# Attention scores in a one-core trunk kernel: two query blocks at a time, each on 64 rows of TensorE, in three products instead of two

## The chip, the cores and the metric

The kernel runs on one core of one Trainium2 chip, in one launch. The metric is the device time of that launch in microseconds (us), lower is better. The engines are named as the profile names them: PE is TensorE's matmul, PEld its weight load, DVE is VectorE, ACT is ScalarE, POOL is GpSimd, SP is the engine whose queue issues the DMAs here.

## The reference, cut to what matters

The model is one layer over a sequence of 2048 rows of width 1024: a wide input projection, a convolution branch, an attention branch of 8 heads of 64, and two output projections. The change lies in the attention branch alone:

```python
z = jnp.einsum("bqhd,bkhd->bhqk", qb, kb, preferred_element_type=jnp.float32) * scale
mask = s_idx < t_idx
log_beta = jax.nn.log_sigmoid(z)
log_1m_beta = jnp.where(mask, log_beta - z, 0.0)
suffix = lax.cumsum(log_1m_beta, axis=3, reverse=True) - log_1m_beta
weights = jnp.where(mask, jnp.exp(log_beta + suffix), 0.0)
outs.append(jnp.einsum("bhqk,bkhd->bqhd", weights.astype(v.dtype), vb))
```

Every score z = q.k is over 64 numbers. The weight of a key is its sigmoid times the product of one minus the sigmoids of the keys between it and the query.

## The kernel before

**Precision.** Every float32 operand is split into a high part (a cast to `float32r`, the matmul format) and a low part (the rest), and a product is made from high times high, high times low and low times high. A dense product (`mm3`) is three matmuls for each 128 rows of contraction.

**Stages.** The first projects the input (x normalised, transposed and split) into q, k, v, the convolution's input and most gates, normalises the heads and writes q and k to DRAM, head by head and in chunks of 512 rows: tiles `qst` and `kst` of 128 x 512, where partitions 0 to 63 hold the high part of the 64 numbers and 64 to 127 the low part. The second stage is the attention, with dense matmuls of the remaining gates put between (the "fill", tile `pd`). The third makes the output projections (tiles `p` and `po`).

**The attention stage.** It goes over 80 units (head h, query chunk rc, key chunk g, with g from rc to 3; the sequence is stored reversed). 32 units are diagonal (g equal to rc), where only the keys from a block's own column on count; 48 are off the diagonal. A unit has four query blocks (qb 0 to 3) of 128 queries, against 512 keys. For each block:

- `z_stage` makes the scores on PE in one PSUM bank (tile `z`, three banks): two matmuls of 128 contraction rows. `q1` holds [high; low] of the queries and `q2` [low; high], both against `kt`, [high; low] of the keys. The first gives high x high + low x low, the second low x high + high x low: all four products. On the diagonal the matmuls are 512, 384, 256 and 256 columns wide for the blocks 0 to 3.
- ACT makes the sigmoid (`w`, seven buffers) and the sigmoid of the negated score (back into `z`), DVE a running product along the keys (`sc`, a scan that reads `z` and so holds its bank), POOL multiplies it into `w`.
- One unit later `av_stage` (called `T(kb)` in the unit's loop) transposes the four `w` of a key block on PE (`pT`), ACT and DVE split them into `thi` and `tlo`, and `av_mm` (`AV(kb)`) multiplies them with the values into `av`.

**What sets the order.** From the stage before on, `pin[0]` is true, and PE keeps the order in which the program calls it. In a unit that order is Z(0), fill, the last AV of the unit before, fill, Z(1), T(3), fill, T(2), fill, Z(2), fill, AV(3), T(1), Z(3), AV(2), T(0), fill, AV(1); `others` puts in as many steps of the fill (three matmuls each) as a table of due times says. ACT, DVE, POOL and the DMA queue of SP are ordered by the scheduler. All loads and stores of the stage are issued by SP, in order.

**Loads.** `load_q` brings q for one (h, rc) by three DMAs, one chunk ahead; two buffers. `kt` and `vt` are loaded at the first query chunk of a head (rc equal to 0) and used by all units of that key chunk.

Of the kernel before, what the change touches and what calls it, by code (L numbers as in the profile page):

```python
# [8 lines left out]
F32 = mybir.dt.float32  # L9
F32R = mybir.dt.float32r  # L10
# [9 lines left out]
P = 128  # L20
# [3 lines left out]
CH = 512  # L24
# [6 lines left out]
HD = 64  # L31
# [15 lines left out]
def f(ap):  # L47
    return ap.bitcast(F32)
# [3 lines left out]
def trunk_kernel(  # L52
# [20 lines left out]
    nc = tc.nc  # L73
# [6 lines left out]
    def dram(name, shape, dt):  # L80
        return dp.tile(shape, dt, name=name, tag=name)
# [27 lines left out]
    def load_piece(pool, src):  # L109
        hi = pool.tile([P, 1024], F32R, tag="whi", name="whi")  # L110
        lo = pool.tile([P, 1024], F32R, tag="wlo", name="wlo")
        split_into(src, hi, lo)
        return hi, lo
# [3 lines left out]
    def mm(*a, **k):  # L117
        i = nc.tensor.matmul(*a, **k)  # L118
        if pin[0]:
            tc.keep_in_program_order(i)  # L120
# [36 lines left out]
    kst_d = [[dram(f"kst{h}_{g}", [P, CH], F32) for g in range(NCH)] for h in range(NH)]  # L157
    qst_d = [[dram(f"qst{h}_{g}", [P, CH], F32) for g in range(NCH)] for h in range(NH)]
# [29 lines left out]
    def hT(g):  # L188
        return hT_[g]
# [10 lines left out]
    with ExitStack() as s1:  # L200
# [221 lines left out]
        with tc.tile_pool(name="hx", reuse_waits="tile", bufs=1) as hx:  # L422
# [88 lines left out]
            for kc in range(KC):  # L511
# [10 lines left out]
                hi, lo = (h[kc] for h in hT(g0))  # L522
# [28 lines left out]
            def first(w2):  # L551
                return [nat_tile(pd, w2, g0, half) for half in range(2)]
# [12 lines left out]
            h = h_chunk(ORDER[1], hx, (), xs)  # L565
# [4 lines left out]
            k1 = first(w2_k1)  # L570
# [5 lines left out]
            h = h_chunk(ORDER[2], hx, (0, 4))  # L576
# [319 lines left out]
    with ExitStack() as s2:  # L896
        at = s2.enter_context(tc.tile_pool(name="at", reuse_waits="tile", bufs=1, side="right"))
        pd = s2.enter_context(tc.tile_pool(name="pd2", reuse_waits="tile", bufs=2, space=PSUM))
        pz = s2.enter_context(tc.tile_pool(name="pz", reuse_waits="tile", bufs=3, space=PSUM))
# [37 lines left out]
        kt, vt = {}, {}  # L937
        st = {}

        def load_q(h, rc):  # L940
            q1 = at.tile([P, CH], F32R, tag="q1", name="q1", bufs=2)
            q2 = at.tile([P, CH], F32R, tag="q2", name="q2", bufs=2)
            nc.sync.dma_start(f(q1), qst_d[h][rc])
            nc.sync.dma_start(f(q2[0:HD]), qst_d[h][rc][HD:P])
            nc.sync.dma_start(f(q2[HD:P]), qst_d[h][rc][0:HD])
            st[h, rc] = {"q": (q1, q2), "w": {}}

        def z_stage(h, rc, g, qb):
            diag = g == rc
            if qb == 0:  # L950
                if rc == 0:
                    kt[g] = at.tile([P, CH], F32R, tag=f"kt{g}", name=f"kt{g}")
                    nc.sync.dma_start(f(kt[g]), kst_d[h][g])
                    vt[g] = at.tile([P, 4, P], F32R, tag=f"vt{g}", name=f"vt{g}")
                    nc.sync.dma_start(f(vt[g]), vst_d[h][g])
                if diag:
                    nxt = (h, rc + 1) if rc + 1 < NCH else (h + 1, 0)
                    for hr in ((h, rc), nxt) if n_ == 0 else (nxt,):
                        if hr[0] < NH:
                            load_q(*hr)  # L960
            s_ = st[h, rc]
            q1, q2 = s_["q"]
            lo = qb * P if diag else 0
            zlo = min(lo, 256)
            qs = slice(qb * P, (qb + 1) * P)
            z = pz.tile([P, CH], F32, tag="z", name="z")
            mm(z[:, zlo:], q1[:, qs], kt[g][:, zlo:], start=True, stop=False)
            mm(z[:, zlo:], q2[:, qs], kt[g][:, zlo:], start=False, stop=True)
            w = at.tile([P, CH], F32, tag="w", name="w", bufs=7)
            nc.scalar.activation(out=w[:, lo:], in_=z[:, lo:], func=AF.Sigmoid, scale=HD ** -0.5)  # L970
            nc.scalar.activation(out=z[:, lo:], in_=z[:, lo:], func=AF.Sigmoid,  # L971
                                 scale=-HD ** -0.5)
            s = sc[qb]
            if not diag:
                nc.vector.tensor_tensor_scan(  # L975
                    out=s[:, 1:], data0=z, data1=w, initial=s[:, 0:1],
                    op0=ALU.mult, op1=ALU.bypass)
            else:
                nc.vector.tensor_tensor_scan(  # L979
                    out=s[:, lo + 1:], data0=z[:, lo:], data1=tri[:, :CH - lo], initial=1.0,  # L980
                    op0=ALU.mult, op1=ALU.max)
            nc.gpsimd.tensor_tensor(out=w[:, lo:], in0=w[:, lo:], in1=s[:, lo:CH], op=ALU.mult)  # L982
            if diag:
                nc.gpsimd.affine_select(
                    out=w[:, lo:lo + P], in_=w[:, lo:lo + P], pattern=[[1, P]],
                    compare_op=ALU.is_gt, fill=0.0, base=0, channel_multiplier=-1)
            if g < NCH - 1:
                nc.gpsimd.tensor_copy(s[:, 0:1], s[:, CH:CH + 1])
            s_["w"][g, qb] = w
# [23 lines left out]
        def av_mm(h, rc, g, kb, v_, n, av, thi, tlo):  # L1013
            mm(av[:, :n], v_[:, kb, :], thi[:, :n],
                             start=(g == rc and kb == 3), stop=False)
            mm(av[:, :n], v_[:, kb, :], tlo[:, :n],
                             start=False, stop=(g == NCH - 1 and kb == 0))
            if g == NCH - 1 and kb == 0:
                lo_, hi_ = slice(0, HD), slice(HD, P)
                a, b = (lo_, hi_) if h % 2 == 0 else (hi_, lo_)  # L1020
                oc = at.tile([P, CH], F32, tag="fsg", name="oc", bufs=2)
                nc.scalar.copy(out=oc[a], in_=av[b])
                nc.vector.tensor_tensor(out=oc[a], in0=av[a], in1=oc[a], op=ALU.add)
                nc.sync.dma_start(o_d[h // 2][rc][a], oc[a])
# [109 lines left out]
        units = [(h, rc, g) for h in range(NH) for rc in range(NCH) for g in range(rc, NCH)]  # L1134
# [26 lines left out]
        for n_, u in enumerate(units + [None]):  # L1161
            r = [None] * 4
            p = prev[0] if prev else None

            def T(kb):
                if p:
                    r[kb] = av_stage(*p, kb, prev[1])

            def AV(kb):
                if p:  # L1170
                    av_mm(*p, kb, prev[1], *r[kb])

            def Z(qb):
                if u is not None:
                    z_stage(*u, qb)

            def others(q, half):

                nonlocal nf, ny, ygen, wr, yp
                while nf < (int(due[2 * q + half + 1] + 0.001) if q < LAST else NF):  # L1180
                    next(fill)
                    nf += 1
                if early and not half:
                    steps, quarter, f_, a = early[0]
                    if (nf >= steps and q % 2 == 0) if quarter == 0 else q >= quarter:
                        early.pop(0)

                        with tc.high_priority(offset=-60):
                            f_(a)
                if q == LAST - 8 and not half:  # L1190
                    wcs[0] = load_piece(wpa, w_cs[0])
                if q == LAST and not half:
                    hst.close()
                    wr = s3.enter_context(tc.tile_pool(name="wr", reuse_waits="tile", bufs=1))
                    yp = s3.enter_context(tc.tile_pool(name="yp", reuse_waits="tile", bufs=1))
                    with tc.high_priority(offset=0):
                        wo[0] = load_piece(wpa, w_out[0])
                    z0_ = [zt[kc] for kc in range(2 * JC)]
                    ygen = y_tiles(0, halves(z0_[:JC]), halves(z0_[JC:]), lambda n: psum(n), y)
                if q >= LAST:  # L1200
                    next(ygen)
                    ny += 1

            Z(0)
            others(4 * n_, 0)
            if held:
                av_mm(*held)
            others(4 * n_, 1)
            Z(1)
            T(3)  # L1210
            others(4 * n_ + 1, 0)
            T(2)
            others(4 * n_ + 1, 1)
            Z(2)
            others(4 * n_ + 2, 0)
            AV(3)
            T(1)
            Z(3)
            AV(2)
            T(0)  # L1220
            others(4 * n_ + 2, 1)
            others(4 * n_ + 3, 0)
            others(4 * n_ + 3, 1)
            AV(1)
            held = (*p, 0, prev[1], *r[0]) if p else None
            prev = (u, vt[u[2]]) if u is not None else None
# [73 lines left out]
```

## Time and profile before

| what | value |
|---|---|
| runs of the kernel before | 1830.12, 1831.95, 1835.28 us, median 1831.95 |
| the profiled execution | 1829.36 us, its span 1827.6 us |
| PE busy, share of the span | 97% |
| attention stage (first to last score) | 783 to 1485 us of the span |
| score matmuls | 640, in 160 pairs of two query blocks |
| DMA over the attention stage | 93 GB/s, mean busy share 0.31 |

How to read it: times in a view are microseconds from the start of the span, single instructions in nanoseconds where a column says ns. A matmul's duration is longer than the time by which it holds up the next one, since matmuls are pipelined and their ends are modelled, so what a matmul costs is read from start to start. "128*128 128x512" is a weight of 128 x 128 and a moving operand of 128 partitions by 512 columns. In the timeline "x2" joins two like instructions, from the start of the first to the end of the last. An arrow "<-" behind an idle time names what ended it.

### The profile page before, as it was taken

The page shows a single profiled execution, that of the slowest core. Times are in us where ns is not written, and L with a number is a line of the kernel's source. Part 1 is how long each engine was busy: PE and PEld are TensorE (multiplying, and loading weights), DVE is VectorE, ACT ScalarE, POOL GpSimd, SP SyncE. Part 2 cuts the span into 40 slices and gives each one's busy share as a digit, 9 for nine tenths or more (in the row PEclk, how much of TensorE's full clock was granted, in tenths as well). Part 3 has the DMA queues.
Part 4 walks back from the last instruction along what each step waited for, and adds up shares of the span by engine and source line. Part 5 has one row for each costly group of instructions (what it writes and reads, how often), then busy time and mean ns, then how long its engine had stood idle before and what let it go on. Part 6 is the DMA issues. An engine that isn't in the chain of part 4 may idle for free.

```text
span 1827.6 us, 27222 instructions
## 1 busy us (share of the span) xinstructions
PE 1773.7 (97%) x9612; PEld 1507.4 (82%) x9612; DVE 1231.1 (67%) x1696; ACT 833.2 (46%) x1960; POOL 659.2 (36%) x819
## 2 busy tenths in 40 slices
PE   6899999999999999999999999999999999999999
PEld 5888889899898888878888888887787777888887
DVE  7656577987879555567777787877778785334341
ACT  5465113222131143367777777777777652010100
POOL 0253112102111133366666666666666721010100
PEclk9999999999999999999999999999999999999999
DMA  8563411415133454342232323232324346353532
GB/s 295 174 190 104 139 35 53 121 37 165 41 101 102 145 179 144 132 133 85 78 100 72 105 72 99 63 100 73 96 76 156 95 136 213 104 162 99 169 95 81
DMA packets 117597, 211.08 MB, mean 115 GB/s; under 512 B 15442, under 2 KB 27730, under 8 KB 117460
## 3 DMA queue, kind: packets, MB, share of 16 engines
q1 hardware_dynamic: 116308, 207.24, 36.8%
q10 hardware_dynamic: 1152, 2.10, 0.3%
q8 instruction: 76, 1.25, 0.3%
q14 instruction: 61, 0.50, 0.1%
HBM read 137.98 MB, written 71.30 MB: 115 GB/s over the span
## 4 chain that ended last, share of the span: by engine, by line
PE 77%; DVE 7%; POOL 4%; issue 4%; DMA 4%; ACT 3%; SPq 0%; ACTq 0%; DVEq 0%; POOLq 0%
PE pd L118 44%; PE po L118 9%; PE p L118 9%; PE av L118 5%; PE pT L123 5%; PE z L118 4%; POOL w L982 3%; DVE sc L975 2%; DVE tlo L1009 1%; ACT z L971 1%; PE pt L123 1%; DMA wl<-in_w_cs_dram 1%; POOL wlo L106 1%; DMA wl<-in_w_qkv_dram 1%; DMA qst<-qhi 1%
## 5 line engine op out<-in xcount | busy, mean ns | idle before, releaser
L982 POOL TENSOR_TENSOR w<-w,sc 128x512 f32<-128x512 f32 (+1 forms) x320 | 362.0, 1133 | 235.0 <-DVE sc L975 175.6
L118 PE MATMUL pd<-hh,whi 128*128 128x512 f32 x1024 | 326.1, 400 | 0.0
L975 DVE TENSOR_TENSOR_SCAN sc<-z,sc,w 128x512 f32<-128x512 f32 x192 | 244.2, 1277 | 74.3 <-ACT z L971 73.5
L106 POOL TENSOR_TENSOR wlo<-wl,whi 128x512 fp32r<-128x512 f32 x88 | 131.6, 1506 | 407.3 <-ACT whi L105 406.3
L970 ACT ACTIVATE w<-z 128x512 f32<-128x512 f32 (+1 forms) x320 | 171.8, 537 | 126.5 <-PE z L118 102.4
L118 PEld LDWEIGHTS pd<-hh,whi 128*128 128x128 f32 x1024 | 183.7, 189 | 31.1
L118 PE MATMUL pd<-hhi,whi 128*128 128x512 f32 x512 | 208.3, 407 | 1.0 <-ACT vsg L882 1.0
L1009 DVE TENSOR_TENSOR tlo<-pT,thi 128x512 fp32r<-128x512 f32 (+1 forms) x320 | 186.0, 598 | 30.0 <-ACT thi L1008 27.0
L118 PE MATMUL pd<-hhi,wlo 128*128 128x512 f32 x512 | 200.4, 391 | 0.0
L118 PE MATMUL pd<-hlo,whi 128*128 128x512 f32 x512 | 200.3, 391 | 0.0
L118 PE MATMUL pd<-hh,wlo 128*128 128x512 f32 x512 | 200.1, 391 | 0.0
L118 PE MATMUL z<-kt,q 128*128 128x512 f32 (+2 forms) x640 | 190.9, 379 | 0.0
L123 PE MATMUL pT<-ident,w 128*128 128x128 f32 x1088 | 174.7, 274 | 7.8 <-POOL w L982 6.2
L1008 ACT CAST thi<-pT 128x512 fp32r<-128x512 f32 (+1 forms) x320 | 165.6, 526 | 36.1 <-PE pT L123 33.0
L123 PEld LDWEIGHTS pT<-ident,w 128*128 128x128 f32 x1088 | 136.7, 140 | 47.2 <-POOL w L982 14.4
L971 ACT ACTIVATE z<-z 128x512 f32<-128x512 f32 (+1 forms) x320 | 171.8, 537 | 0.0
L979 DVE TENSOR_TENSOR_SCAN sc<-z,tri 128x512 f32<-128x512 f32 (+3 forms) x128 | 104.3, 820 | 58.4 <-ACT z L971 38.0
L105 ACT CAST whi<-wl 128x512 fp32r<-128x512 f32 x88 | 53.8, 623 | 163.9 <-PE pd L118 135.4
L118 PE MATMUL av<-tlo,vt 128*128 128x512 f32 (+1 forms) x320 | 120.3, 376 | 8.2 <-DVE tlo L1009 7.8
L118 PEld LDWEIGHTS z<-kt,q 128*128 128x128 f32 x640 | 109.7, 189 | 14.7 <-DVE sc L979 0.3
L118 PE MATMUL av<-thi,vt 128*128 128x512 f32 (+1 forms) x320 | 116.7, 365 | 0.0
L118 PEld LDWEIGHTS pd<-hhi,wlo 128*128 128x128 f32 x512 | 96.4, 188 | 20.9
(289 smaller groups left out, 3553.6 us busy)
## 6 DMA issues: line engine op xcount, KB each, us to landing
wl<-in_w_in_dram SPq DMA_DIRECT2D x64, 256.0 KB, 3.0
wa<-in_w_ada_dram SPq DMA_DIRECT2D x24, 512.0 KB, 5.5
wl<-in_w_qkv_dram SPq DMA_DIRECT2D x36, 256.0 KB, 2.8
xt<-in_x_n_dram SPq DMA_DIRECT2D x16, 512.0 KB, 5.5
vst<-st SPq DMA_DIRECT2D x64, 128.0 KB, 2.0
kt<-kst SPq DMA_DIRECT2D x32, 256.0 KB, 2.8
vt<-vst SPq DMA_DIRECT2D x32, 256.0 KB, 2.6
q<-qst SPq DMA_DIRECT2D x32, 256.0 KB, 2.9
```

The source lines that it names most:

```text
L105: nc.scalar.copy(out=hi[:, s], in_=wl)
L106: (lo_eng or nc.gpsimd).tensor_tensor(out=lo[:, s], in0=wl, in1=f(hi[:, s]), op=ALU.subtract)
L118: i = nc.tensor.matmul(*a, **k)
L123: i = nc.tensor.transpose(*a)
L970: nc.scalar.activation(out=w[:, lo:], in_=z[:, lo:], func=AF.Sigmoid, scale=HD ** -0.5)
L971: nc.scalar.activation(out=z[:, lo:], in_=z[:, lo:], func=AF.Sigmoid, scale=-HD ** -0.5)
L975: nc.vector.tensor_tensor_scan(out=s[:, 1:], data0=z, data1=w, initial=s[:, 0:1], op0=ALU.mult, op1=ALU.bypass)
L979: nc.vector.tensor_tensor_scan(out=s[:, lo + 1:], data0=z[:, lo:], data1=tri[:, :CH - lo], initial=1.0, op0=ALU.mult, op1=ALU.max)
L982: nc.gpsimd.tensor_tensor(out=w[:, lo:], in0=w[:, lo:], in1=s[:, lo:CH], op=ALU.mult)
L1008: nc.scalar.copy(out=thi[:, :n], in_=pT[:, :n])
L1009: nc.vector.tensor_tensor(out=tlo[:, :n], in0=pT[:, :n], in1=f(thi[:, :n]), op=ALU.subtract)
```

## The change

Scores are made for two query blocks at once (`z_pair(a)`, blocks 2a and 2a+1), each by three matmuls of 64 contraction rows: high x high, high x low (of the keys), low x high. The product low x low is left out. The first block of a pair works from partitions 0 to 63, the second from 64 to 127: in the built program each of these matmuls is marked with a tile of 64 rows at row 0 or row 64, where all others use 128 rows.

For that, q is laid out anew: `qh` holds the high parts and `ql` the low parts, with the even blocks of 128 queries on partitions 0 to 63 and the odd ones on 64 to 127; each is loaded by two DMAs in runs of 128 numbers (four DMAs for each (h, rc) instead of three). Next to `kt` ([high; low]) the keys are also loaded the other way round as `k2` ([low; high]), by two DMAs of 64 x 512 for each of the 80 units, one unit ahead, in two buffers. The matmuls of a pair alternate between the two banks and between the two halves.

In the unit's order Z(0) now makes blocks 0 and 1 where block 0 was made, Z(1) blocks 2 and 3 where block 2 was made. The two matmuls of a pair's second block are as wide as before, in three instead of two products. What follows the scores is unchanged.

```diff
         def load_q(h, rc):
-            q1 = at.tile([P, CH], F32R, tag="q1", name="q1", bufs=2)
-            q2 = at.tile([P, CH], F32R, tag="q2", name="q2", bufs=2)
-            nc.sync.dma_start(f(q1), qst_d[h][rc])
-            nc.sync.dma_start(f(q2[0:HD]), qst_d[h][rc][HD:P])
-            nc.sync.dma_start(f(q2[HD:P]), qst_d[h][rc][0:HD])
-            st[h, rc] = {"q": (q1, q2), "w": {}}
-
-        def z_stage(h, rc, g, qb):
+
+            qs = []
+            for i, n in enumerate(("qh", "ql")):
+                q = at.tile([P, 2, P], F32R, tag=n, name=n, bufs=2)
+                src = qst_d[h][rc][i * HD:(i + 1) * HD].rearrange("p (a b c) -> p a b c", a=2,
+                                                                  b=2)
+                for b in range(2):
+                    nc.sync.dma_start(f(q[b * HD:(b + 1) * HD]), src[:, :, b, :])
+                qs.append(q)
+            st[h, rc] = {"q": qs, "w": {}}
+
+        k2s = {}
+
+        def load_k2(u):
+
+            k2 = at.tile([P, CH], F32R, tag="k2", name="k2", bufs=2)
+            nc.sync.dma_start(f(k2[0:HD]), kst_d[u[0]][u[2]][HD:P])
+            nc.sync.dma_start(f(k2[HD:P]), kst_d[u[0]][u[2]][0:HD])
+            k2s[u] = k2
+
+        def z_pair(h, rc, g, a):
             diag = g == rc
-            if qb == 0:
+            if a == 0:
...
                     for hr in ((h, rc), nxt) if n_ == 0 else (nxt,):
                         if hr[0] < NH:
                             load_q(*hr)
+                if n_ == 0:
+                    load_k2(units[0])
+                if n_ + 1 < len(units):
+                    load_k2(units[n_ + 1])
+            qh, ql = st[h, rc]["q"]
+            k1, k2 = kt[g], k2s[h, rc, g]
+            zs = [pz.tile([P, CH], F32, tag="z", name="z") for _ in range(2)]
+            for i, q in enumerate((qh, qh, ql)):
+                for b in range(2):
+                    r = slice(b * HD, (b + 1) * HD)
+                    lo = min((2 * a + b) * P if diag else 0, 256)
+                    mm(zs[b][:, lo:], q[r, a, :], (k1, k2)[(i + b) % 2][r, lo:],
+                       start=i == 0, stop=i == 2)
+            for b in range(2):
+                z_stage(h, rc, g, 2 * a + b, zs[b])
+
+        def z_stage(h, rc, g, qb, z):
+            diag = g == rc
             s_ = st[h, rc]
-            q1, q2 = s_["q"]
             lo = qb * P if diag else 0
-            zlo = min(lo, 256)
-            qs = slice(qb * P, (qb + 1) * P)
-            z = pz.tile([P, CH], F32, tag="z", name="z")
-            mm(z[:, zlo:], q1[:, qs], kt[g][:, zlo:], start=True, stop=False)
-            mm(z[:, zlo:], q2[:, qs], kt[g][:, zlo:], start=False, stop=True)
             w = at.tile([P, CH], F32, tag="w", name="w", bufs=7)
...
             others(4 * n_, 1)
-            Z(1)
             T(3)
             others(4 * n_ + 1, 0)
             T(2)
             others(4 * n_ + 1, 1)
-            Z(2)
+            Z(1)
             others(4 * n_ + 2, 0)
             AV(3)
             T(1)
-            Z(3)
             AV(2)
             T(0)
```

The order of the built programs on PE is shown at two places of the same unit: an off-diagonal unit (key chunk 3), around the second half of its scores. Before the change (`q` are `q1` and `q2`, `kt` the keys, `pd` the fill, `pT` the transposes of the unit before, `av` its output):

```order
L123 MATMUL pT<-ident,w 128x128 x4
L118 MATMUL z<-kt_10120,q_9697 128x512
L118 MATMUL z<-kt_10120,q_9698 128x512
L118 MATMUL pd<-hhi_0_1716,whi 128x512
L118 MATMUL pd<-hlo_0_1724,whi 128x512
L118 MATMUL pd<-hhi_0_1716,wlo 128x512
L118 MATMUL av<-thi,vt_10019 128x512
L118 MATMUL av<-tlo,vt_10019 128x512
L123 MATMUL pT<-ident,w 128x128 x4
L118 MATMUL z<-kt_10120,q_9697 128x512
L118 MATMUL z<-kt_10120,q_9698 128x512
```

The same place with the change (`k` is `k2`):

```order
L123 MATMUL pT<-ident,w 128x128 x4
L118 MATMUL z<-kt_10294,qh 128x512
L118 MATMUL z<-k_10188,qh 128x512 x2
L118 MATMUL z<-kt_10294,qh 128x512
L118 MATMUL z<-kt_10294,ql 128x512
L118 MATMUL z<-k_10188,ql 128x512
L118 MATMUL pd<-hhi_0_1716,whi 128x512
L118 MATMUL pd<-hlo_0_1724,whi 128x512
L118 MATMUL pd<-hhi_0_1716,wlo 128x512
L118 MATMUL av<-thi,vt_10186 128x512
L118 MATMUL av<-tlo,vt_10186 128x512
L123 MATMUL pT<-ident,w 128x128 x4
```

Four score matmuls of 128 rows, two and two, became six of 64 rows in one piece, between a transpose of 128 rows ahead of them and a dense matmul of 128 rows behind them.

The second place is SP's queue of DMA issues at the start of the attention stage. Before the change, from the store of a fill's result on (`mb`), with the loads of q for the second query chunk behind it:

```order
L932 DMA mb1_0_239<-fsg_7747 128x512
L943 DMA q1_7788<-qst0_1_104 128x512
L944 DMA q2_7789<-qst0_1_104 64x512
L945 DMA q2_7789<-qst0_1_104 64x512
L953 DMA kt1_7852<-kst0_1_72 128x512
```

With the change, from the same store on:

```order
L932 DMA mb1_0_239<-fsg_7747 128x512
L948 DMA qh_7789<-qst0_1_104 64x2x128 x2
L948 DMA ql_7792<-qst0_1_104 64x2x128 x2
L957 DMA k2_7795<-kst0_0_71 64x512
L958 DMA k2_7795<-kst0_0_71 64x512
L957 DMA k2_7798<-kst0_1_72 64x512
L958 DMA k2_7798<-kst0_1_72 64x512
L966 DMA kt1_7864<-kst0_1_72 128x512
```

The first unit's `k2`, which its first scores read, stands behind that store and behind four loads of q that belong to a later unit.

More of the change, by code (lines that the diff above doesn't have):

```diff
@@ L1171, in AV, with Z @@
                     av_mm(*p, kb, prev[1], *r[kb])
-            def Z(qb):
+            def Z(a):
                 if u is not None:
-                    z_stage(*u, qb)
+                    z_pair(*u, a)
             def others(q, half):
```

## The prediction

> **What bounds the kernel now.** I read the page first, then the busy time by stretches, then the score matmuls by shape, then the timeline of PE and PEld where scores are made.
>
> ```profile
> span 1827.6 us, 27222 instructions
> PE 1773.7 (97%) x9612; PEld 1507.4 (82%) x9612; DVE 1231.1 (67%) x1696; ACT 833.2 (46%) x1960; POOL 659.2 (36%) x819
> PE 77%; DVE 7%; POOL 4%; issue 4%; DMA 4%; ACT 3%; SPq 0%; ACTq 0%; DVEq 0%; POOLq 0%
> core 0: us, PE busy (x) PEld busy (x) DVE busy (x) ACT busy (x) POOL busy (x), PEclk, DMA share, GB/s
> 0.00:783.00 783.00, 750.30 (x4501) 666.69 (x4502) 543.92 (x804) 259.43 (x735) 180.49 (x137) 1.00 0.41 128
> 783.00:1485.00 702.00, 686.00 (x3619) 562.13 (x3618) 549.41 (x693) 527.53 (x1146) 460.92 (x666) 1.00 0.31 93
> ```
>
> PE is the bound: 686 of the 702 us of the attention stage, and 77% of the chain that ended last. In that stage DVE is busy 549 us, ACT 528, POOL 461, DMA 0.31, at a full clock (1.00). So time taken from PE there comes off the span until DVE's 549 us is near, and time added to PE is added to the span. The term to get right is what PE pays for the scores:
>
> ```profile
> L118 PE MATMUL z<-kt,q 128*128 128x512 f32 x448 | 145.4, 406 | 0.0
> L118 PE MATMUL z<-kt,q 128*128 128x256 f32 x128 | 29.1, 309 | 0.0
> L118 PE MATMUL z<-kt,q 128*128 128x384 f32 x64 | 16.3, 336 | 0.0
> ```
>
> These durations overlap (each contains the way of the data in and the results out), so the cost is taken from start to start:
>
> ```profile
> 1011.81 0.39 PE L118 MATMUL av<-tlo,vt 128*128 128x512 f32 x1
> 1012.04 0.61 PE L118 MATMUL z<-kt,q 128*128 128x512 f32 x2
> 1012.49 0.62 PE L118 MATMUL pd<-hh,whi 128*128 128x512 f32 x2
> ...
> 1002.93 0.28 PE L118 MATMUL av<-thi,vt 128*128 128x256 f32 x1
> 1003.04 0.28 PE L118 MATMUL av<-tlo,vt 128*128 128x256 f32 x1
> 1003.16 0.40 PE L118 MATMUL z<-kt,q 128*128 128x512 f32 x1
> ...
> 1013.62 0.51 PE L118 MATMUL z<-kt,q 128*128 128x384 f32 x2
> 1013.97 0.27 PE L123 MATMUL pT<-ident,w 128*128 128x128 f32 x1
> ...
> 1006.35 0.60 PE L123 MATMUL pT<-ident,w 128*128 128x128 f32 x4
> ```
>
> A matmul of 512 columns holds up the next by 0.45 / 2, about 227 ns; of 384 by 0.35 / 2 = 175; of 256 by (1003.16 - 1002.93) / 2 = 115. Its own duration is 390, so its end lies 390 - 227 = 163 ns behind the start of the next. The four transposes carry a weight load each and follow each other by (600 - 274) / 3 = 109 ns, 274 being the second `pT` row's 0.27: a weight load of 128 columns occupies PEld for at most 110 ns. And when does a load begin?
>
> ```profile
> 1012.94 0.39 PE L118 MATMUL pd<-hh,wlo 128*128 128x512 f32 x1
> 1012.95 0.19 PEld L118 LDWEIGHTS av<-thi,vt 128*128 128x128 f32 x1
> 1013.17 0.39 PE L118 MATMUL av<-thi,vt 128*128 128x512 f32 x1
> 1013.17 0.19 PEld L118 LDWEIGHTS av<-tlo,vt 128*128 128x128 f32 x1
> 1013.40 0.39 PE L118 MATMUL av<-tlo,vt 128*128 128x512 f32 x1
> ```
>
> As the matmul before its own starts, never earlier: loads run one ahead.
>
> **The change part by part.**
>
> *Six matmuls of 64 rows for four of 128.* No row shows two matmuls at once, so it is bounded. If the halves run at once but loads go one ahead, the second half starts a load (110 ns) behind the first, and a half repeats every 227 ns: off the diagonal the pair takes 2 x 227 + 110 + 227 = 791 ns instead of 4 x 227 = 908, a gain of 117. There are 48 x 2 = 96 such pairs: 11.2 us. On the diagonal the first pair (512 and 384 wide) takes 2 x 227 + 110 + 175 = 739 for 2 x 227 + 2 x 175 = 804, gain 65; the second is 256 wide, where two loads (220) outlast a matmul (115): five steps of 110 and a last 115 make 665 for 4 x 115 = 460, a loss of 205. Net loss 140 x 32 diagonal units = 4.5 us. Sum: a gain of 6.7 us. If the second load is not held back, an off-diagonal pair takes 3 x 227 = 681 (gain 21.8 us), a diagonal unit loses 205 - 123 = 82 (2.6 us): gain 19.2. If both halves load at once, the 256-wide pair takes 345 too and the gain is 21.8 + (123 + 115) x 32 = 29.4. If the halves do not run at once, three products cost 1.5 times two: 48 x 908 and 32 x (402 + 230), half of 804 and of 460, make a loss of 43.6 + 20.2 = 63.8. I take 6.7, since the loads above are always one ahead.
>
> *Switching between 128 and 64 rows.* Each of 160 pairs stands between instructions of 128 rows, so PE switches 320 times. No row shows a switch. A matmul of 128 rows is still passing the lower half when the next starts; if the next uses the halves apart, PE may have to let the first run out. The price lies between 0 (a transpose after a matmul, also another kind of pass, starts without a gap in these rows) and the 163 ns by which an end lies behind the next start; with a load (110) only begun after it, 273. I take 120, between half of 163 and all of it, since part of a duration is the way in, which the next can overlap: 320 x 0.12 = 38.4 us, all on PE. The range uses 80 to 163, that is 25.6 to 52.2 us. The Trainium skill (TensorEngine Tiling (Array Packing), Key Properties) states that changing the tiling mode, not just the tile, drains TensorE, and gives no price. No run here shows it yet; by that rule the switch costs something, and without it the sum would be the gain alone.
>
> *The start of the stage.* The first unit's `k2` goes out behind a store and four loads of q.
>
> ```profile
> 780.08 0.33 SPq L932 DMA_DIRECT2D mb<-fsg  x1
> 780.45 0.43 SPq L943 DMA_DIRECT2D q<-qst  x1
> 780.92 0.47 SPq L944 DMA_DIRECT2D q<-qst  x1
> 783.34 0.62 PE L118 MATMUL z<-kt,q 128*128 128x512 f32 x2
> q<-qst SPq DMA_DIRECT2D x60, 128.0 KB, 3.0
> ```
>
> The store holds the queue until 780.4; four loads at 0.48 end at 782.4, the second half of `k2` issues at 782.9 and lands 3.0 us later, at 785.9, where PE wanted its first scores at 783.3. PE keeps its order, so the fill behind them waits too: 2.5 us, once. It is between 0 and 5.
>
> *Loads and queue after that.* `k2` adds 160 issues and q 32, at about 0.5 us each: some 95 us of SP in 702. They add 80 x 256 KB = 21 MB, or 30 GB/s, to 93; the first stage above runs at 128. A load goes out when the unit before the last has read its buffer, more than half a unit (702 / 80 = 8.8 us) ahead, and takes 3. Nothing on the path; what queues behind a waiting `k2` on SP are stores and loads for later units.
>
> *Two banks at once, of three.* A pair needs the bank of the pair before's first block, held until its scan has read it.
>
> ```profile
> 1080.61 0.62 PE L118 MATMUL z<-kt,q 128*128 128x512 f32 x2
> 1082.52 1.29 DVE L975 TENSOR_TENSOR_SCAN sc<-z,sc,w 128x512 f32<-128x512 f32 x1 [2.15 <-ACT z L971]
> 1084.82 0.62 PE L118 MATMUL z<-kt,q 128*128 128x512 f32 x2
> ```
>
> Block 0 starts at 1080.61, its scan ends at 1083.81; block 2, where the next pair now stands, starts at 1084.82. Block 0 is finished some 0.3 us later in a pair, so 0.7 us is left: hidden by the fill and transposes between. Were that gone, 0.3 us at each of 160 pairs would be 48 us. The `w` of block 3 still waits for T(0), as now. Costed at nothing.
>
> *Sum.* 1829.36 - 6.7 + 38.4 + 2.5 = 1863.6 us against the profiled execution. The median of the runs is 2.6 us above that execution, so the forecast for a median is 1866.2.
>
> **The rivals.**
>
> *No price for the switch: faster.* The halves run at once, both loads go out ahead, a switch costs nothing. It decides at (19.2 - 2.5) / 320 = 52 ns a switch: below that the change gains. It gives 1831.95 - 19.2 + 2.5 = 1815.3, with loads at once 1805.1, with loads one ahead 1827.8. For it: transposes and matmuls alternate without a gap; against it: nothing shows that rows can be re-divided while a matmul is under way. The Trainium skill (the same page and section) has tiles execute LdWeights and Matmul in parallel; no run here shows it, and by that rule alone the 1805 end is the one.
>
> *Small price, no difference.* Between 35 and 69 ns a switch the 16.7 us of that gain (19.2 - 2.5) are used up to within 0.3% (5.5 us, about what a measurement of this kernel can tell from no change): 1826.5 to 1837.4.
>
> *The halves do not run at once.* Then the change does not do what it says: 1831.95 + 63.8 + 2.5 = 1898.3 without any price for switching. For it: the three products are half as much again of PE's instructions (960 for 640 score matmuls); against it: they name different rows and different banks.
>
> *The loads wait for the emptied array too.* 320 x 0.273 = 87.4: 1831.95 - 6.7 + 87.4 + 2.5 = 1915.2.
>
> **How the numbers follow.** The switch with a price of 80 to 163 ns: 0.41, with 1853.4 to 1880.0 of its own. No price: 0.33. No difference: 0.11. Halves one after the other: 0.09. Loads behind the emptying: 0.06. So faster by over 0.3% is 0.33, within 0.3% is 0.11, slower is 0.41 + 0.09 + 0.06 = 0.56. Both signs hold much, so the range is wide: from 1811, which leaves out the best part of the faster case (0.07), to 1898, which leaves out the last case and half of the one before (0.10).
>
> **What would show it.** In the timeline of the changed kernel, the six score matmuls: starts in twos, or 110 ns apart, mean that the halves run at once; starts 227 apart that they don't. From the start of the matmul before a pair to the pair's first I expect 227 + 120, and as much too long from the pair's last to the fill behind it; 227 in both places makes the switch free and the forecast wrong. PE's stage from the first score to the last should last 34 us longer than 702, the stages around it the same. The first scores should begin in time but stop for `k2` for some 2.5 us. A wait of PE on DVE's scan before a pair would mean that the banks decide.

## The result, and the profile after

The changed kernel takes 1879.71 us (median of four runs, 1876.10 to 1882.26) where the kernel before takes 1831.15. The ratio is 1.026, interval 1.025 to 1.027: slower by 48.5 us. The profiled execution took 1880.88 us, its span is 1879.2.

The head of the page, and the busy time in the stretches before the first score, from the first to the last score, and after it. The columns of the stretches are the length in us and then the busy time of PE, PEld, DVE, ACT and POOL, with the number of their instructions; the last three are the granted clock of PE, the busy share of the DMA engines and GB/s:

```profile
span 1879.2 us, 28038 instructions
PE 1812.6 (96%) x9932; PEld 1476.3 (79%) x9932; DVE 1222.5 (65%) x1696; ACT 833.1 (44%) x1960; POOL 656.8 (35%) x819
0.00:785.20 785.20, 755.19 (x4503) 672.08 (x4503) 544.21 (x804) 259.61 (x735) 180.89 (x137) 0.99 0.40 128
785.20:1533.10 747.90, 717.57 (x3925) 524.04 (x3926) 539.03 (x688) 525.49 (x1142) 454.56 (x663) 1.00 0.34 105
1533.10:1879.20 346.10, 339.83 (x1510) 280.22 (x1506) 139.31 (x205) 48.02 (x85) 21.37 (x20) 1.00 0.44 131
```

The last two stretches of the kernel before, with the same bounds:

```profile
783.30:1484.70 701.40, 685.40 (x3616) 561.58 (x3616) 549.11 (x692) 527.28 (x1145) 460.62 (x666) 1.00 0.31 93
1484.70:1827.60 342.90, 337.72 (x1498) 278.83 (x1496) 138.10 (x201) 46.47 (x80) 18.09 (x17) 1.00 0.44 132
```

Nearly all of the time came in the attention stage: 747.9 us, against 701.4. Of the 51.6 us between the two spans 1.9 lie ahead of it and 3.2 behind it; some 2 of these 3.2 only changed sides, because the last score now stands earlier in its unit's order, with one AV, one T and a step of the fill more behind it. DVE, ACT and POOL do there what they did. DMA went from 93 to 105 GB/s and stayed far from full.

The price can be read off the timeline of one pair off the diagonal; first PE, then PEld:

```profile
1040.89 0.39 PE L118 MATMUL av<-tlo,vt 128*128 128x512 f32 x1
1041.21 0.49 PE L118 MATMUL z<-kt,qh 64*128 64x512 f32 x1
1041.21 0.72 PE L118 MATMUL z<-k,qh 64*128 64x512 f32 x2
1041.55 0.39 PE L118 MATMUL z<-kt,qh 64*128 64x512 f32 x1
1041.78 0.39 PE L118 MATMUL z<-kt,ql 64*128 64x512 f32 x1
1041.78 0.39 PE L118 MATMUL z<-k,ql 64*128 64x512 f32 x1
1042.11 0.73 PE L118 MATMUL pd<-hh,whi 128*128 128x512 f32 x2
1042.68 0.39 PE L118 MATMUL pd<-hh,wlo 128*128 128x512 f32 x1
```

```profile
1040.67 0.19 PEld L118 LDWEIGHTS av<-tlo,vt 128*128 128x128 f32 x1
1041.21 0.18 PEld L118 LDWEIGHTS z<-kt,qh 64*128 64x128 f32 x1 [0.35 <-issue]
1041.21 0.29 PEld L118 LDWEIGHTS z<-k,qh 64*128 64x128 f32 x2
...
1041.55 0.18 PEld L118 LDWEIGHTS z<-kt,ql 64*128 64x128 f32 x1
1041.55 0.18 PEld L118 LDWEIGHTS z<-k,ql 64*128 64x128 f32 x1
1042.10 0.30 PEld L118 LDWEIGHTS pd<-hh,whi 128*128 128x128 f32 x2 [0.37 <-issue]
```

Four things are to be seen. The two halves run at once: the matmuls start in twos (1041.21 and 1041.21, 1041.78 and 1041.78), and so do their weight loads. Inside the run a pair of products takes what one takes, 1041.78 - 1041.55 = 0.23 us. At each end of the run there is a gap: from the last `av` to the first score 0.32 instead of 0.227, from the last score to the fill 0.33, so some 95 ns each (98 and 96 by the medians over all pairs). I call this gap the emptying; the trace shows its length, not what happens in it. And the first weight load on each side begins only behind that gap, together with its matmul (1041.21, 1042.10; PEld idle 0.35 and 0.37, "issue"), where in the kernel before a load begins as the matmul ahead of its own starts. So the load is not hidden either: the first two products are 0.34 apart instead of 0.23, and the two `pd` behind the run last 0.73 from end to end instead of 0.62.

Over all pairs, from starts in this trace (medians by shape, from the last instruction ahead to the second behind, less what these cost by themselves): 1105 ns off the diagonal, 1098 and 758 on it, where the old products cost 908, 804 and 460. Three products at no price would be 681, 681 and 345. So the fewer products save 96 x 0.227 + 32 x (0.123 + 0.115) = 29.4 us, and two switches a pair cost 67 us (0.21 each): a loss of 37.8.

The waits of PE in that stage, first in the kernel before, where these are all that last over 1 us, then the four longest in the changed kernel:

```profile
PE av L118 <- DVE tlo L1009: 7.8, 16, 1.9
PE pT L123 <- POOL w L982: 6.2, 8, 3.2
```

```profile
PE av L118 <- DVE oc L1048: 13.4, 11, 1.6
PE av L118 <- DVE tlo L1034: 8.2, 16, 1.2
PE z L118 <- DMA k<-kst: 2.4, 1, 2.4
PE z L118 <- DVE sc L1000: 2.3, 1, 2.3
```

`oc` is the copy that empties the output bank `av` before the next query chunk may use it; `k<-kst` is the first unit's `k2`. PE waited for a score bank (`sc`) once; the weight loads of the scores waited for one eleven times, 6.3 us in all with that one.

### The profile page after: what moved, and what is told of

It reads as the page before. It is cut to its first block, busy times and chain, and to the rows that moved or that the text cites. A ratio compares the mean times of both kernels' runs of the same rounds, so it can differ in the third digit from the quotient of the medians.

```text
span 1879.2 us, 28038 instructions
## 1 busy us (share of the span) xinstructions
PE 1812.6 (96%) x9932; PEld 1476.3 (79%) x9932; DVE 1222.5 (65%) x1696; ACT 833.1 (44%) x1960; POOL 656.8 (35%) x819
## 3 DMA queue, kind: packets, MB, share of 16 engines
q8 instruction: 78, 1.28, 0.3%
## 4 chain that ended last, share of the span: by engine, by line
PE 79%; DVE 8%; ACT 3%; issue 3%; DMA 3%; POOL 2%; SPq 1%; DVEq 0%; ACTq 0%; POOLq 0%
PE pd L118 45%; PE po L118 9%; PE p L118 8%; PE av L118 6%; PE z L118 6%; PE pT L123 5%; DVE sc L1000 3%; DVE tlo L1034 1%; ACT z L996 1%; PE pt L123 1%; DMA wl<-in_w_qkv_dram 1%; POOL w L1007 1%; DMA qst<-qhi 1%; DMA wl<-in_w_out_dram 1%; DVE oc L1048 1%
## 5 line engine op out<-in xcount | busy, mean ns | idle before, releaser
L118 PE MATMUL pd<-hh,whi 128*128 128x512 f32 x1024 | 332.4, 406 | 0.0
L1000 DVE TENSOR_TENSOR_SCAN sc<-z,sc,w 128x512 f32<-128x512 f32 x192 | 239.5, 1275 | 119.4 <-ACT z L996 117.7
L118 PE MATMUL pd<-hhi,whi 128*128 128x512 f32 x512 | 214.2, 418 | 1.0 <-ACT vsg L882 1.0
L118 PEld LDWEIGHTS pd<-hh,whi 128*128 128x128 f32 x1024 | 179.8, 189 | 44.9 <-issue 15.4
L123 PE MATMUL pT<-ident,w 128*128 128x128 f32 x1088 | 168.7, 273 | 0.4 <-POOL w L1007 0.2
L118 PE MATMUL av<-thi,vt 128*128 128x512 f32 (+1 forms) x320 | 130.1, 407 | 17.1 <-DVE oc L1048 13.4
L118 PEld LDWEIGHTS pd<-hhi,whi 128*128 128x128 f32 x512 | 97.0, 189 | 31.8 <-issue 14.5
L118 PE MATMUL z<-k,qh 64*128 64x512 f32 (+2 forms) x320 | 108.6, 417 | 4.6 <-DMA k<-kst 2.4
```

The source lines that it names most:

```text
L123: i = nc.tensor.transpose(*a)
L1000: nc.vector.tensor_tensor_scan(out=s[:, 1:], data0=z, data1=w, initial=s[:, 0:1], op0=ALU.mult, op1=ALU.bypass)
```

## The experiments

Theory A: the loss is the price of changing between 128 and 64 rows, about 0.2 us, 320 times. Theory B: it is the new order, which wants two blocks' scores at once.

**The new order with the old products.** `z_pair` in the changed places, with `q1`, `q2` and no `k2` (shown against the changed kernel):

```diff
-            for i, q in enumerate((qh, qh, ql)):
+            for i, q in enumerate(st[h, rc]["q"]):
                 for b in range(2):
-                    r = slice(b * HD, (b + 1) * HD)
-                    lo = min((2 * a + b) * P if diag else 0, 256)
-                    mm(zs[b][:, lo:], q[r, a, :], (k1, k2)[(i + b) % 2][r, lo:],
-                       start=i == 0, stop=i == 2)
+                    qb = 2 * a + b
+                    lo = min(qb * P if diag else 0, 256)
+                    mm(zs[b][:, lo:], q[:, qb * P:(qb + 1) * P], kt[g][:, lo:],
+                       start=i == 0, stop=i == 1)
```

> The scores of two blocks in one piece and at the changed places, but each by the two old products of 128 rows from q1 and q2; no k2. Theory A (each switch between 128 and 64 rows costs PE about 205 ns: 95 of emptying and 110 of a weight load that no longer hides, 320 times): the time of the kernel before, 1831 us, within 6. Theory B (the loss is the new order: two banks wanted at once, ACT and DVE bunched, the copy of the output behind them): near the changed kernel, 1870 to 1880.

Measured: 1846.45 us, ratio to the kernel before 1.0075 (1.006 to 1.009). Neither theory: the order costs some 14 us of the 48, and most of the rest is the 64 rows (the first `k2` is tried apart below). Its stage and its longest wait of PE:

```profile
785.50:1499.00 713.50, 684.59 (x3606) 558.49 (x3606) 538.01 (x687) 525.00 (x1141) 457.76 (x663) 1.00 0.30 91
PE av L118 <- DVE oc L1029: 14.9, 14, 1.5
```

PE is as busy as before (684.6 for 685.4 us), and waits for `oc`, for which the kernel before did not wait at all.

**More switches for the same work.**

```diff
+            nonlocal nf
             for i, q in enumerate((qh, qh, ql)):
+                if i == 2 and nf < NF:
+                    next(fill)
+                    nf += 1
                 for b in range(2):
```

> The changed kernel with one step of the fill (three matmuls of 128 rows that it would do elsewhere) put between the second and the third product of every pair: the same work, 640 switches instead of 320. Theory A: 320 x 0.205 = 66 us more, 1945. Theory B: no more than a few us beside 1880.

Measured: 1972.53 us, ratio 1.076 (1.074 to 1.078), 93 us above the changed kernel instead of 66. The split pairs (154 of them; the fill ran out for six) cost by their starts 868 and 638 ns for 1105, 401 for two switches: 62 us. The rest is cover taken away: the steps of the fill no longer stand ahead of the AVs. By PE's starts 151 AVs come directly behind a score instead of 53, and the AVs start some 30 us later in all, with the switch ahead of them taken off. A part of it has a name in the waits; that for `oc` went from 13.4 to

```profile
PE av L118 <- DVE oc L1052: 23.6, 28, 1.0
```

**64 rows off the diagonal only.** With the weights taken from `q1` and `q2`, whose halves hold the same parts:

```diff
+            for i, q in enumerate(() if diag else ((q1, q2), (q1, q2), (q2, q1))):
+                for b in range(2):
+                    r = slice(b * HD, (b + 1) * HD)
+                    c0 = (2 * a + b) * P
+                    mm(zs[b], q[b][r, c0:c0 + P], (kt[g], k2s[h, rc, g])[(i + b) % 2][r],
+                       start=i == 0, stop=i == 2)
+            for i, q in enumerate((q1, q2) if diag else ()):
...
```

> 64 rows and three products only in the 48 off-diagonal units, the 32 diagonal ones by the two old products in the new order; q laid out as before, k2 in one buffer. 192 switches. Theory A: by the medians of the changed trace a diagonal unit's two pairs cost 294 and 298 ns more than before, so 32 x 0.592 = 19 us less than 1880: 1861. Theory B: the order is that of the changed kernel everywhere, so 1875 to 1880.

Measured: 1870.83 us, ratio 1.021 (1.019 to 1.022), 9 us less than the changed kernel instead of 19. The direction is theory A's. The size is spoilt by the single buffer of `k2` that this kernel has room for, which it shares with `kt0`. Ahead of the instructions on `k2` the engines (weight loads and matmuls added up) sat idle until:

```profile
  DMA k<-kst: 9.8, 15
```

In the changed kernel the same row has 5.0 us, 2 times. By the starts of the matmuls 13 pairs were late for `k2` by 9.6 us in all, against one pair and 2.9 us: 6.7 of the 10 us that are missing.

**One half for both blocks.**

```diff
-                    r = slice(b * HD, (b + 1) * HD)
+                    r = slice(0, HD)
...
-                    mm(zs[b][:, lo:], q[r, a, :], (k1, k2)[(i + b) % 2][r, lo:],
+                    mm(zs[b][:, lo:], q[r, a, :], (k1, k2)[i % 2][r, lo:],
```

> The changed kernel with both blocks of a pair taken from rows 0 to 63 (the odd blocks then get the even blocks' scores): the same switches, but no two matmuls on different rows. If the halves run at once in the changed kernel, as the starts 3 ns apart say, three matmul times come on top per pair: 96 x 0.681 + 32 x 0.525 + 32 x 0.345 = 93 us, 1973. If those starts were only stamps, nothing: 1880.

Measured: 1948.19 us, one run, 68 us more. Products that were together are now one after the other: by their starts a run lasts 689 ns longer off the diagonal, 587 and 355 on it, 96 us in all, with the same gaps at its ends. So the starts in twos were real, and the gaps belong to the 64 rows, not to running two at once. The 28 us that are missing are in the main waits that it saved: PE's idle time in the stage fell from 30.3 to 10.1 us, and that for `oc` from 13.4 to

```profile
PE av L118 <- DVE oc L1048: 3.3, 9, 0.7
```

**The output's copy first.** The first run had brought up a third theory, C: the copy and the sum that empty `av` stand behind both blocks of a pair, where before they stood behind one. At the same place of the work, first in the kernel before, then in the changed kernel:

```profile
876.72 0.58 ACT L1022 COPY oc<-av 64x512 f32<-64x512 f32 x1
876.80 1.28 DVE L975 TENSOR_TENSOR_SCAN sc<-z,sc,w 128x512 f32<-128x512 f32 x1 [2.54 <-ACT z L971]
878.00 0.66 DVE L1023 TENSOR_TENSOR oc<-av,oc 64x512 f32<-64x512 f32 x1
879.42 0.39 PE L118 MATMUL av<-thi,vt 128*128 128x512 f32 x1
```

```profile
887.46 2.46 DVE L1000 TENSOR_TENSOR_SCAN sc<-z,sc,w 128x512 f32<-128x512 f32 x2 [3.09 <-ACT z L996]
888.89 0.58 ACT L1047 COPY oc<-av 64x512 f32<-64x512 f32 x1
...
889.83 1.13 DVE L1034 TENSOR_TENSOR tlo<-pT,thi 128x512 fp32r<-128x512 f32 x2
...
890.88 0.67 DVE L1048 TENSOR_TENSOR oc<-av,oc 64x512 f32<-64x512 f32 x1
...
891.70 0.47 PE L118 MATMUL av<-thi,vt 128*128 128x512 f32 x1 [1.28 <-DVE oc L1048]
```

Before, one scan stands ahead of the sum, and the next AV comes 0.76 us behind it without a wait. Now it is two scans in one piece, two `tlo` behind them, only then the sum, and PE idle 1.28 us for it. Of the 32 sums of each kernel 30 stand behind one scan before and 30 behind two now.

```diff
-                nc.scalar.copy(out=oc[a], in_=av[b])
-                nc.vector.tensor_tensor(out=oc[a], in0=av[a], in1=oc[a], op=ALU.add)
+                with tc.high_priority(offset=60):
+                    nc.scalar.copy(out=oc[a], in_=av[b])
+                    nc.vector.tensor_tensor(out=oc[a], in0=av[a], in1=oc[a], op=ALU.add)
```

In the changed kernel:

> The changed kernel with a higher priority for the copy and the sum that empty the output bank (oc), so that on DVE they stand ahead of the scan of a pair's second block instead of behind it. Theory C (the new order costs 13 us because that copy now stands behind two blocks' work and the next chunk's first AV waits for its bank): 1880 less 10 to 13, 1867 to 1870. Theory C' (the order costs through something else, the wait only changes its name): 1877 to 1882.

Measured: 1872.96 us, ratio 1.0224 (1.0210 to 1.0238), 6.8 us less. In the new order with the old products:

> The new order with the old products (as in e1_pair_order) and the output's copy ahead. Theory C: the 13 us of e1_pair_order go, 1833 to 1836; if the pair order also saves waits of the transposes for POOL (14 us before, 7 in e1_pair_order), a little below the kernel before. Theory C': 1844 to 1848.

Measured: 1837.61 us, ratio 1.0035 (1.0022 to 1.0047), 8.8 us less than without (7.3 by the two ratios). In both the wait for `oc` fell to 1.4 us, but that for `tlo`, which the sum now stands ahead of, rose; in the second:

```profile
786.70:1493.50 706.80, 685.08 (x3606) 559.68 (x3605) 538.74 (x687) 524.30 (x1141) 456.89 (x663) 1.00 0.29 92
PE av L118 <- DVE tlo L1015: 14.0, 27, 1.4
PE av L118 <- DVE oc L1030: 1.4, 2, 0.8
```

So the wait partly changed its name, as theory C' has it, and theory C holds for about half of the order's loss. PE's idle time ahead of the transposes, most of it for POOL, did fall (7.8 us before, 3.2 here), but no version of the new order beat the old one. What the last 6 us of it are was not tried; in the profiles 5.4 us lie in the stage (706.8 for 701.4), and 3.4 already ahead of the first score.

**The first k2 first.**

```diff
                     nc.sync.dma_start(f(vt[g]), vst_d[h][g])
+                if n_ == 0:
+                    load_k2(units[0])
                 if diag:
```

and the later call gone.

> The changed kernel with the first unit's k2 issued ahead of the loads of q instead of behind the store and four of them. If the first scores' stop of some 3 us is on the path: 1877, and no stop in the timeline. If the fill makes up for it later: 1880.

Measured: 1874.49 us, ratio 1.0233 (1.0220 to 1.0247), 5.2 us less, more than the stop. The stop in the changed kernel, on PE and on SP:

```profile
785.17 0.50 PE L118 MATMUL z<-kt,qh 64*128 64x512 f32 x1
788.03 0.50 PE L118 MATMUL z<-k,qh 64*128 64x384 f32 x2 [2.36 <-DMA k<-kst]
```

```profile
782.20 1.18 SPq L948 DMA_DIRECT2D qh<-qst  x2
783.42 1.25 SPq L948 DMA_DIRECT2D ql<-qst  x2
784.71 0.60 SPq L957 DMA_DIRECT2D k<-kst  x1
785.36 0.59 SPq L958 DMA_DIRECT2D k<-kst  x1
```

The second product waits 2.9 us for the half of `k2` issued at 785.36. With `k2` first the six matmuls start within 0.63 us (785.71 to 786.34). The stop has a sequel, first in the changed kernel, then with `k2` first:

```profile
788.60:792.00 3.40, 3.40 (x11) 2.17 (x10) 1.98 (x2) 2.11 (x5) 0.67 (x1) 0.50 0.92 301
788.60:792.00 3.40, 2.92 (x15) 2.02 (x15) 2.36 (x4) 1.52 (x5) 2.73 (x5) 1.00 0.87 220
```

For 3.4 us behind the stop PE is granted half its clock (0.50), and the matmuls of the fill start 0.43 us apart instead of 0.227. A stretch at 0.50 begins within 2 us of the stop in all four kernels of this document whose PE is idle there for `k2` for 1.5 to 2.6 us, and there is none at that place in the other eight. By the second pair the changed kernel has lost 3.9 us against this one, counted from the first score of each, and 3.0 to 3.3 of them stay to the middle of the stage. So the stop and its sequel explain some 3 us. The rest of the 5 is open: it comes late in the stage in the two profiles, where other stretches at half clock fall at different times, and the intervals of the two ratios nearly touch.

**Both mended.** The two edits together.

> The changed kernel with both the output's copy ahead on DVE and the first k2 ahead on SP. If the two are separate losses they add: 1880 - 7 - 5 = 1868, and what is left above e7_order_output_first (1837.6), 30 us, is the 64 rows themselves: 320 switches at 0.20 us less 29 us of fewer products. If one only moves the other's wait: 1872 to 1874.

Measured: 1869.23 us, ratio 1.0201 (1.0187 to 1.0215). They add, but for some 1.5 us. What is left above the same order with the old products is 1869.2 - 1837.6 = 31.6 us: the 64 rows with their loads, near the 37.8 of the pairs' starts. Those were set against the steady 908, 804 and 460 ns; the same reading of the old pairs in the new order (the first experiment's trace) gives 931, 820 and 484, and so 34 us and 0.20 us a switch.

**The price alone.** Two short matmuls of 64 rows ahead of each pair of the new order with the old products:

```diff
+            for b in range(2):
+                r = slice(b * HD, (b + 1) * HD)
+                mm(zs[b][:, 256:], q1[r, 0:P], kt[g][r, 256:], start=True, stop=True)
```

> e1_pair_order with two matmuls of 64 rows and 256 columns put ahead of each pair's old products (they write what the first old product then overwrites): 320 switches with no gain to set against. Theory A: by the two-matmul pieces in e2_more_switches, 529 ns each, 160 x 0.53 = 85 us on top of 1846: 1931. If a switch were free the two would cost 115 ns together: 1865; as two matmuls of 128 rows 230 ns: 1883.

Measured: 1907.91 us, ratio 1.041 (1.040 to 1.043), 61.5 us above that kernel. By their starts the pieces cost 518 ns each (median), as expected, 83 us in all; the 20 us or so that do not show in the time took the place of waits (PE's idle time in the stage fell from 28.9 to 17.2 us, the part for `oc` from 14.9 to 8.5). Of the 518, 115 are the two matmuls themselves at once, so a switch costs (518 - 115) / 2 = 201 ns with no gain beside it.

**Half the weights.** The same with `q1[r, 0:HD]` as weights and `zs[b][0:HD, 256:]` as output.

> e8_price_alone with weights of 64 columns in the two added matmuls (their output has 64 partitions). Theory A (of a switch's 200 ns, 110 are the weight load that starts only when the array is empty): the entry's load halves, the first dense matmul behind does not change: 518 - 55 = 463 ns a piece, 160 x 0.055 = 9 us less than e8's 1908: 1899. If the 200 ns are all emptying, whatever is loaded: 1908.

Measured: 1900.49 us, ratio 1.0375 (1.0361 to 1.0390), 7.4 us less; the pieces cost 463 ns (median), 55 less. One piece of each kernel, first with full, then with half weights:

```profile
1021.50 0.40 PE L118 MATMUL av<-tlo,vt 128*128 128x512 f32 x1
1021.82 0.39 PE L118 MATMUL z<-kt,q 64*128 64x256 f32 x2
1022.14 0.74 PE L118 MATMUL z<-kt,q 128*128 128x512 f32 x2
```

```profile
1018.52 0.40 PE L118 MATMUL av<-tlo,vt 128*128 128x512 f32 x1
1018.85 0.33 PE L118 MATMUL z<-kt,q 64*64 64x256 f32 x2
1019.11 0.51 PE L118 MATMUL z<-kt,q 128*128 128x512 f32 x1
```

The gap ahead is the same (0.32 and 0.33, though the tile is 64*64 now), the piece itself is 0.26 instead of 0.32: the load of 64 columns takes half of 110 ns, in plain sight. So a switch is a gap of some 95 ns, the emptying, and a weight load that starts only after it.

## Why the prediction was right, and which of its terms were not

The direction, the place and the mechanism in the main were right: the halves run at once, the switch costs more than the fewer products save, on PE and in the attention stage, and 1879.7 lies in the range, at the upper end of the likeliest case's own (1853.4 to 1880.0). The sign named for the stage, 34 us more, came out at 46.5. Term by term:

- *Fewer products: 6.7 us forecast, 29.4 found.* The step that failed is "I take 6.7, since the loads above are always one ahead". That rule of the trace held between weights that all use the same rows; loads for different halves start together, so the upper bound was the right one. The sentence of the Trainium skill (TensorEngine Tiling (Array Packing), Key Properties) on tiles that execute LdWeights and Matmul in parallel is what the trace shows, 1041.21 twice.
- *The switch: 0.12 us forecast, 0.20 to 0.21 found, 64 to 67 us instead of 38.4.* The emptying was put too high and the load left out: 95 ns, not 120, but 110 more for the load, on both sides. The forecast had that case as a rival ("the loads wait for the emptied array too"), at 0.273 with a chance of 0.06; its mechanism was right and its emptying too long. The Trainium skill (TensorEngine Tiling (Array Packing), Key Properties) states that a change of tiling mode drains TensorE. The trace agrees with it, with a gap of 95 ns at each change, and adds the price.
- These two errors, 23 us one way and 26 to 29 the other, nearly cancel: 38.4 - 6.7 = 31.7 us were forecast for the 64 rows, and the runs gave 31.6. That this sum is right is luck, since neither of its terms is.
- *The start of the stage: 2.5 us forecast, 2.9 of stop in the trace, 5.2 off the time.* Right in place. Every issue on SP there, of q and of `k2`, took 0.6 us and not 0.48, and the half clock behind the stop was in no term.
- *Two banks at once, "costed at nothing".* For the banks this was nearly right: 6.3 us of waits of the weight loads, 2.3 of PE. But only the scores' own waits were considered. The new order put two blocks' work on ACT and DVE ahead of the copy that frees the output bank, and that cost about half of the 14 us that no term held; the other half has no cause shown. These 14 us are nearly the whole distance of the forecast, 1866.2, from 1879.7.
- *Loads and queue after the start*: nothing, as said; two buffers of `k2` sufficed where one did not.

The terms as measured, 34 to 38 by the starts, 14 and 5, make 53 to 57, more than the 48.5 of the whole: PE's gaps and PE's waits cover each other, as the pieces that cost 83 us and moved the time by 61.5 showed.

## What to carry to other kernels

Row tiling pays by the run, not by the matmul: a run of 64-row matmuls between 128-row ones costs two switches, here 0.41 us, and each pair of blocks saves 0.227, so by these figures a run must hold two pairs before it gains at all (an estimate; no run here holds two). When work is bunched to serve one engine, look at what the other engines' queues now hold ahead of a step that frees a buffer. A rule read from a trace ("loads go one ahead") holds for the kind of instruction that the trace has.

## What the runs showed of the hardware

- Two `float32r` matmuls of 64 x 128 x 512 on different row halves take 0.23 us together, as one of 128 rows does.
- A change between matmuls of 128 and of 64 rows leaves a gap of some 95 ns, and the first weight load behind it is not issued ahead: 110 ns for 128 columns, 55 less for 64. The price did not change with running one half alone.
- A stop of PE of 1.5 to 2.6 us for `k2` at the start of the stage was followed within 2 us by 3.4 us or more at half the granted clock (0.50) each time it came, in four kernels.
- Issuing a DMA of q in runs of 128 numbers held SP's queue for at least 0.52 us (medians 0.55 and 0.59), a DMA of 64 whole rows for at least 0.44 (medians 0.45 to 0.59) and one of q with 128 whole rows for 0.32. The 0.6 us of both kinds at the start of the stage are thus not the price of the short runs.
